# New duration estimates for TensorE and ScalarE in a kernel that orders its own instructions

## The chip, the cores and the metric

The kernel runs on one core of one Trainium2 chip, in one launch. The metric is the device time of a launch in microseconds (us). TensorE (PE) does the matrix products, VectorE (DVE), ScalarE (ACT) and GpSimd (POOL) the elementwise work, and SyncE (SP) issues the transfers. Each engine works through its own instructions in the order in which they were emitted, so an instruction that waits holds up all that stands behind it on its engine.

## The reference, cut to what matters

One layer of a hybrid encoder runs over 1104 rows: 16 meta rows and 1024 frames of a prompt, and 64 rows of a second request group with a cache of 272 rows. D_MODEL is 1024, D_FF 2816.

```
x = x + 0.5 * (silu(rmsnorm(x) @ wg) * (rmsnorm(x) @ wu)) @ wd     # feed-forward 1
p = rmsnorm(x) @ w_in                                              # one projection, split among the heads
# group A: gated DeltaNet, 4 heads: short convolution + silu, l2-normalised q and k,
#   per chunk: u = solve(I + a, rhs); o = eg*(q@m0) + (q k^T * decay)@u; m = exp(g)*m0 + k^T@u
# group B: latent attention, 4 heads: cq = rmsnorm(p_q) @ w_uq, c = rmsnorm(p_kv), rotary parts,
#   keys and values from c @ w_ukv, softmax over a block-causal mask
x = x + concat(A, B) @ w_out
x = x + 0.5 * (silu(rmsnorm(x) @ wg) * (rmsnorm(x) @ wu)) @ wd     # feed-forward 2
y = rmsnorm(x)                                                     # final norm
```

All inputs and outputs are float32.

## The kernel before

**Numbers.** A float32 product is made of three passes over operands that are cut in a high part and a remainder (names that end in h and l, as wh and wl): high by high, remainder by high, high by remainder. ScalarE casts the high part, VectorE subtracts to get the remainder. The rows of x are handled in four blocks of 276 columns or three of 384, 384 and 336. In the feed-forwards the products go by a scheme of seven products for eight (class `Seven`): sums and differences of two pairs of weight blocks and of two pairs of activation blocks (tiles `raw`, `wx`; `s`, `st`) are formed by VectorE first, and TensorE's results are added up into several banks' worth of output (`sn`, `hb`).

**Stages.** Feed-forward 1: `norm_pair` prepares the activations of pair 0 and pair 1 while the first weights arrive, then the gate and up products run (`half_steps`, in cycles of 14 blocks of 12 products with 276 columns), their silu product `hb` is written to DRAM (`hd`) and comes back, split, as `XH` and `XL` for the products with wd. Then a norm (`norm_chunk`), the combined projection head by head (`head_proj`), the delta rule in groups of three chunks (`gdn_group`, tiles like `Zg`, `Tpg`, `T2g`, `Ung` and the state `M`), the latents (`proj_latent`), the queries (`mla_queries`, `query_rope` with tile `qt`), attention (`mla_attend`), the out projection (`out_proj`), feed-forward 2, and the final norm (`final_chunk`, with output tile `fy`).

**What sets the order.** All of these are generators that are registered as tasks with a rank. `Tasks.step` (L468) emits a piece of one task at a time: the first task in order of rank whose planned ready time is not later than the planned time of TensorE, or, if none is ready, the one that gets ready first. The planned times come from `Clock`: `note` (L361) is called after every operation (all are issued from one line, L424, by `Timed`), takes the operands' planned ends plus a latency, and adds `cost` (L351), an estimate of its duration by engine and number of elements. `lag` and `complete` give a task the planned time at which a tile is ready, so a task can ask to go on when it is. Tiles are taken from rings of buffers, and a planned time is kept for when each comes free. Nothing of this exists when the kernel runs: the plan only decides in which order the instructions stand on each engine, and semaphores do the waiting.

Each name carries a number in the order of allocation (`raw_165`, `bk_14159`; `bk` is a bank of PSUM). The numbers differ between the two kernels even where the work is the same. Group tiles carry head and group: `Tpg00` is head 0, group 0.

Of the kernel before, what the change touches and what calls it, by code (L numbers as in the profile page):

```python
# [9 lines left out]
F32R = mybir.dt.float32r  # L10
# [302 lines left out]
class Clock:  # L313
# [37 lines left out]
    def cost(self, eng, op, out, ins):  # L351
        n = max(math.prod(x.shape[1:]) for x in ins + [out])
        if eng == "tensor":
            n = math.prod(out.shape[1:])
            k = 2 if self.at["tensor"] < 6.8 else 1
            if op == "transpose":
                return 0.11 * k
            return k * (max(0.107, n * 0.00042) if ins[-1].dtype == F32R else 2 * max(0.107, n * 0.00084))
        return {"vector": 0.07 + n * 0.00105, "scalar": 0.13 + n * 0.00075, "gpsimd": 0.15 + n * 0.0022}[eng]

    def note(self, eng, op, args, kw):  # L361
        aps = [x for x in list(args) + list(kw.values()) if hasattr(x, "tensor")]
# [2350 lines left out]
```

## Time and profile before

| what | value |
|---|---|
| time, median of 3 runs | 2364.56 us (2363.49 to 2367.12) |
| the profiled execution's own time | 2365.06 us |
| its span | 2363.3 us |
| PE busy | 2299.7 us, 97%, 16356 instructions |
| DVE busy | 1511.4 us, 64%, 3499 instructions |
| ACT busy | 926.4 us, 39%, 2038 instructions |
| POOL busy | 204.3 us, 9%, 488 instructions |
| chain that ended last | PE 85%, DVE 9%, ACT 2%, DMA 2% |
| transfers | 214.29 MB, 91 GB/s on the mean |

The span is that of the profiled execution on the chip; busy is the time in which at least one instruction of an engine is recorded. TensorE is busy for all but 63.6 us of the span. The granted clock of TensorE was 0.985 of full speed over the span. Matmuls are pipelined, so the duration in a row is that from start to result, and a single product shows more (290 ns) than the distance at which products follow each other.

### The profile page before, as it was taken

The page shows a single profiled execution, that of the slowest core. Times are in us where ns is not written, and L with a number is a line of the kernel's source. Part 1 is how long each engine was busy: PE and PEld are TensorE (multiplying, and loading weights), DVE is VectorE, ACT ScalarE, POOL GpSimd, SP SyncE. Part 2 cuts the span into 40 slices and gives each one's busy share as a digit, 9 for nine tenths or more (in the row PEclk, how much of TensorE's full clock was granted, in tenths as well). Part 3 has the DMA queues.
Part 4 walks back from the last instruction along what each step waited for, and adds up shares of the span by engine and source line. Part 5 has one row for each costly group of instructions (what it writes and reads, how often), then busy time and mean ns, then how long its engine had stood idle before and what let it go on. Part 6 is the DMA issues. An engine that isn't in the chain of part 4 may idle for free.

```text
span 2363.3 us, 41362 instructions
## 1 busy us (share of the span) xinstructions
PE 2299.7 (97%) x16356; PEld 2273.8 (96%) x16356; DVE 1511.4 (64%) x3499; ACT 926.4 (39%) x2038; POOL 204.3 (9%) x488
## 2 busy tenths in 40 slices
PE   9999999999999999899998999899999999999998
PEld 8999999999999899899998998899999999999998
DVE  7844554575766767788867566567544554657676
ACT  5433333352112445555533555334333333441123
POOL 0000000000000403323245000000000000000002
PEclk9999999999999999999998999999999999999999
DMA  6322222362421331112122103623222222444212
GB/s 199 112 78 83 83 69 70 101 206 97 142 92 37 114 92 40 55 38 66 36 73 66 45 16 91 194 91 107 80 75 83 83 66 73 147 160 147 87 56 76
DMA packets 231043, 214.29 MB, mean 91 GB/s; under 512 B 18372, under 2 KB 202864, under 8 KB 230848
## 3 DMA queue, kind: packets, MB, share of 16 engines
q1 hardware_dynamic: 230832, 211.64, 28.4%
q8 instruction: 128, 2.10, 0.4%
q14 instruction: 67, 0.55, 0.1%
q10 hardware_dynamic: 16, 0.00, 0.0%
HBM read 159.05 MB, written 52.55 MB: 90 GB/s over the span
## 4 chain that ended last, share of the span: by engine, by line
PE 85%; DVE 9%; ACT 2%; DMA 2%; issue 1%; POOL 1%; SPq 0%; DVEq 0%; ACTq 0%; POOLq 0%
PE bk L424 85%; DVE s L424 1%; DVE cv L424 1%; DVE wl L424 1%; DVE rs_q L424 1%; DMA X<-in_w_out_dram 1%; DVE rs_r L424 0%; ACT wh L424 0%; POOL rs_q L424 0%; ACT s L424 0%; DMA s<-in_w_out_dram 0%; DVE st L424 0%; ACT pp L424 0%; POOL tkq L424 0%; DMA wx<-in_ffn_wg_dram 0%
## 5 line engine op out<-in xcount | busy, mean ns | idle before, releaser
L424 PE MATMUL bk<-s,wh 128*128 128x276 f32 x3136 | 600.9, 290 | 4.9 <-ACT sn L424 2.3
L424 PEld LDWEIGHTS bk<-s,wh 128*128 128x128 f32 x3136 | 492.9, 188 | 6.3 <-ACT sn L424 2.5
L424 PE MATMUL bk<-s,wl 128*128 128x276 f32 x1568 | 449.3, 290 | 1.6 <-DVE wl L424 1.6
L424 PE MATMUL bk<-s,wx 128*128 128x276 f32 x2964 | 394.0, 290 | 1.7 <-DVE s L424 1.7
L424 PEld LDWEIGHTS bk<-s,wx 128*128 128x128 f32 x2964 | 383.5, 188 | 1.9 <-DVE s L424 1.9
L424 DVE SCALAR_TENSOR_TENSOR R<-bk,R 128x384 f32<-128x384 f32 (+1 forms) x480 | 230.6, 533 | 133.4 <-PE bk L424 133.1
L424 PEld LDWEIGHTS bk<-s,wl 128*128 128x128 f32 x1568 | 293.3, 188 | 2.3 <-DVE wl L424 2.3
L424 DVE TENSOR_TENSOR sn<-bk,sn 128x276 f32<-128x276 f32 x237 | 105.1, 444 | 207.5 <-PE bk L424 203.5
L424 ACT COPY sn<-bk 128x276 f32<-128x276 f32 x237 | 92.0, 389 | 243.3 <-PE bk L424 239.2
L424 PE MATMUL bk<-XH,wh 128*128 128x384 f32 (+1 forms) x576 | 166.9, 344 | 0.0
L424 PE MATMUL bk<-XL,wh 128*128 128x384 f32 (+1 forms) x576 | 161.5, 334 | 0.0
L424 PE MATMUL bk<-XH,wl 128*128 128x384 f32 (+1 forms) x576 | 161.5, 334 | 0.0
L424 DVE TENSOR_TENSOR raw<-wx,raw 128x512 f32<-128x512 f32 x40 | 27.6, 691 | 155.1 <-DMA raw<-in_ffn_wu_dram 155.1
L424 ACT CAST wh<-wx 128x512 fp32r<-128x512 f32 (+1 forms) x89 | 76.4, 858 | 100.5 <-DVE wx L424 87.7
L424 DVE TENSOR_TENSOR wx<-raw,wx 128x512 fp32r<-128x512 f32 (+2 forms) x149 | 112.0, 755 | 4.9 <-ACT wx L424 4.8
L424 ACT ACTIVATE sn<-sn 128x276 f32<-128x276 f32 x158 | 68.5, 435 | 117.0 <-DVE sn L424 116.9
L424 PEld LDWEIGHTS bk<-XH,wh 128*128 128x128 f32 x576 | 105.8, 191 | 0.0
L424 PEld LDWEIGHTS bk<-XL,wh 128*128 128x128 f32 x576 | 105.8, 191 | 0.0
L424 PEld LDWEIGHTS bk<-XH,wl 128*128 128x128 f32 x576 | 105.4, 191 | 0.0
L424 DVE TENSOR_TENSOR wl<-raw,wh 128x512 fp32r<-128x512 f32 (+4 forms) x95 | 89.8, 949 | 13.5 <-ACT wh L424 13.4
L424 ACT CAST wh<-raw 128x512 fp32r<-128x512 f32 (+4 forms) x95 | 77.1, 814 | 52.0 <-PE bk L424 28.7
L424 DVE TENSOR_TENSOR wl<-wx,wh 128x512 fp32r<-128x512 f32 (+1 forms) x89 | 87.2, 980 | 12.2 <-ACT wh L424 12.2
(436 smaller groups left out, 4465.3 us busy)
## 6 DMA issues: line engine op xcount, KB each, us to landing
raw<-in_ffn_wu_dram SPq DMA_DIRECT2D x102, 256.0 KB, 4.5
wx<-in_ffn_wg_dram SPq DMA_DIRECT2D x49, 512.0 KB, 4.0
hd<-hb SPq DMA_DIRECT2D x88, 276.0 KB, 2.2
raw<-in_ffn_wd_dram SPq DMA_DIRECT2D x40, 512.0 KB, 4.7
XH<-hd SPq DMA_DIRECT2D x24, 552.0 KB, 3.7
XL<-hd SPq DMA_DIRECT2D x20, 552.0 KB, 4.6
xa<-x SPq DMA_DIRECT2D x16, 552.0 KB, 5.3
raw<-in_w_in_dram SPq DMA_DIRECT2D x16, 512.0 KB, 4.1
```

What stands on the lines that cost most here:

```text
L424: r = f(*args, **kw)
```

## The change

Two lines in `Clock.cost` are altered: for a product with one operand in the fast float32 format, n columns were put at max(0.107, 0.00042 n) us and are now put at max(0.112, 0.0087 + 0.000435 n); for a plain float32 product the floor goes from 0.107 to 0.112, taken twice; an operation of ScalarE with n elements goes from 0.13 + 0.00075 n to 0.14 + 0.00082 n. The estimates of VectorE (0.07 + 0.00105 n), GpSimd, the transfers and all latencies stay.

```
             if op == "transpose":
                 return 0.11 * k
-            return k * (max(0.107, n * 0.00042) if ins[-1].dtype == F32R else 2 * max(0.107, n * 0.00084))
-        return {"vector": 0.07 + n * 0.00105, "scalar": 0.13 + n * 0.00075, "gpsimd": 0.15 + n * 0.0022}[eng]
+            return k * (max(0.112, 0.0087 + n * 0.000435) if ins[-1].dtype == F32R else 2 * max(0.112, n * 0.00084))
+        return {"vector": 0.07 + n * 0.00105, "scalar": 0.14 + n * 0.00082, "gpsimd": 0.15 + n * 0.0022}[eng]
```

The instructions are the same but for a few small products of TensorE that fill the first microseconds (14276 rows before, 14283 now). Their order changes on every engine. Three pieces of it follow, each of before and of now.

VectorE at the start, where the second pair of activations (`s112`, `s113`) is made, before:

```order
127 L424 TENSOR_TENSOR wx2_144<-wx3_145,wx1_143 128x512
128 L424 TENSOR_TENSOR raw_165<-wx3_145,raw_164 128x512
129 L424 TENSOR_TENSOR s112_1258<-st1_116,s15_1206 128x1104
130 L424 TENSOR_TENSOR sn_1237<-bk_1187,sn_1237 128x276
131 L424 TENSOR_TENSOR sn_1251<-bk_1210,sn_1251 128x276
132 L424 TENSOR_TENSOR raw_164<-raw_164 128x512
133 L424 TENSOR_TENSOR wl_163<-wx3_145,wh_162 128x1024
134 L424 TENSOR_TENSOR s113_1291<-st0_115,s16_1260 128x1104
```

and now:

```order
127 L424 TENSOR_TENSOR wx2_144<-wx3_145,wx1_143 128x512
128 L424 TENSOR_TENSOR s112_1227<-st1_116,s15_1158 128x1104
129 L424 TENSOR_TENSOR s113_1259<-st0_115,s16_1229 128x1104
130 L424 TENSOR_TENSOR sn_1243<-bk_1193,sn_1243 128x276
131 L424 TENSOR_TENSOR sn_1257<-bk_1209,sn_1257 128x276
132 L424 TENSOR_TENSOR raw_165<-wx3_145,raw_164 128x512
133 L424 TENSOR_TENSOR raw_164<-raw_164 128x512
134 L424 TENSOR_TENSOR wl_163<-wx3_145,wh_162 128x1024
```

Both activations have moved ahead of the subtraction of raw_164 from wx3_145, a pair of loaded weights.

ScalarE at the end of the gate and up products of feed-forward 1, where the last weights (rA2, rL2) and the first blocks for wd (XH0) come in, before:

```order
335 L424 ACTIVATE sn_4747<-sn_4747 128x276
336 L424 ACTIVATE sn_4767<-sn_4767 128x276
337 L424 CAST wh_158<-rA2_4960 128x1024
338 L424 CAST XH0_4962<-raw_165 128x512
339 L424 CAST XH0_4962<-wx3_145 128x512
340 L424 CAST wx0_142<-raw_164 128x512
341 L424 COPY sn_4988<-bk_4975 128x276
342 L424 COPY sn_5007<-bk_4994 128x276
343 L424 COPY sn_5022<-bk_4975 128x276
```

and now:

```order
339 L424 ACTIVATE sn_4774<-sn_4774 128x276
340 L424 CAST wx0_142<-raw_164 128x512
341 L424 COPY sn_4992<-bk_4979 128x276
342 L424 COPY sn_5011<-bk_4998 128x276
343 L424 COPY sn_5025<-bk_4979 128x276
...
347 L424 CAST XH0_4972<-raw_165 128x512
348 L424 CAST XH0_4972<-wx3_145 128x512
349 L424 CAST wx0_142<-raw_165 128x512
350 L424 COPY sn_5104<-bk_5091 128x276
351 L424 CAST wh_162<-rA2_4970 128x1024
```

The cast from rA2 has moved behind the copies from the banks, ten places down.

VectorE in a cycle of the dense steps of feed-forward 1, where `hb` empties two banks and `raw_165<-wx3_145,raw_164` is the first subtraction of a new block of weights, before:

```order
182 L424 TENSOR_TENSOR wl_161<-raw_164,wh_160 128x512
183 L424 TENSOR_TENSOR wl_161<-wx3_145,wh_160 128x512
184 L424 TENSOR_TENSOR wx3_145<-wx3_145 128x512
185 L424 TENSOR_TENSOR hb_1752<-bk_1612,sn_1625 128x276
186 L424 TENSOR_TENSOR hb_1768<-bk_1632,sn_1645 128x276
187 L424 TENSOR_TENSOR wx2_144<-raw_165,wx1_143 128x512
188 L424 TENSOR_TENSOR wx2_144<-wx3_145,wx1_143 128x512
189 L424 TENSOR_TENSOR wx0_142<-raw_164,wx0_142 128x512
190 L424 TENSOR_TENSOR raw_165<-wx3_145,raw_164 128x512
```

and now:

```order
204 L424 TENSOR_TENSOR wx2_144<-raw_165,wx1_143 128x512
205 L424 TENSOR_TENSOR wx2_144<-wx3_145,wx1_143 128x512
206 L424 TENSOR_TENSOR sn_1875<-bk_2016,sn_1875 128x276
207 L424 TENSOR_TENSOR raw_165<-wx3_145,raw_164 128x512
208 L424 TENSOR_TENSOR raw_164<-raw_164 128x512
209 L424 TENSOR_TENSOR wl_163<-wx3_145,wh_162 128x1024
210 L424 TENSOR_TENSOR hb_1980<-bk_1844,sn_1857 128x276
211 L424 TENSOR_TENSOR wx0_142<-raw_165,wx0_142 128x512
212 L424 TENSOR_TENSOR hb_1996<-bk_1862,sn_1875 128x276
```

The first subtraction of the new block and the wide low part behind it (`wl` of 1024 columns) now stand ahead of the two evacuations `hb<-bk`, where they stood behind them; the subtractions for `wx2` have moved ahead of it all, among the adds into `sn`.

Elsewhere, in words: in the delta rule of head 0, group 0, TensorE has 57 products of 336 columns between its product from `Zg00` and the first from `Tpg00`, where it had 24, and VectorE has one convolution (`cv`) less between the two. At the last solve (head 3, group 2) products of the latents now stand between the steps of the solve (6 between those with `Tfg` and `Xg`, 9 up to `T2g`, 9 up to `U2g`, 6 up to `Ung`), where 18 products of the queries stood in one place and none in the others; 3, 6, 9 and then no query products follow between the steps of the state `M`. In the final norm, where 48 small transposes stood behind the last product of feed-forward 2, 36 of them now stand ahead of its last 12 products.

## Rows read from the trace of the kernel before

**Rows 1.** Stretches of the span: us, busy us (xcount) of each engine, PEclk, DMA, GB/s.

```profile
110.00:455.00 345.00, 345.00 (x2709) 345.00 (x2708) 175.44 (x328) 129.28 (x258) 0.00 (x0) 1.00 0.25 76
800.00:1000.00 200.00, 190.32 (x1196) 187.16 (x1195) 139.54 (x429) 100.16 (x252) 53.61 (x120) 0.94 0.20 61
1000.00:1250.00 250.00, 247.10 (x1781) 243.70 (x1780) 196.83 (x713) 123.47 (x370) 85.60 (x248) 0.99 0.17 52
1250.00:1320.00 70.00, 60.15 (x384) 55.69 (x384) 49.57 (x169) 29.34 (x84) 30.79 (x65) 0.88 0.26 78
```

**Rows 2.** Timeline of PE: start, us, instruction [idle before, what ended it].

```profile
107.29 1.66 PE L424 MATMUL bk<-s,wx 128*128 128x276 f32 x11 [1.71 <-DVE s L424]
462.95 0.53 PE L424 MATMUL bk<-s,wh 128*128 128x276 f32 x2 [2.25 <-ACT sn L424]
908.44 0.82 PE L424 MATMUL bk<-Tpg,V32g 128*128 128x32 f32 x3 [2.91 <-DVE Tpg L424]
978.63 0.49 PE L424 MATMUL bk<-M,wTg 128*128 128x128 f32 x2 [1.46 <-DVE M L424]
1254.36 0.99 PE L424 MATMUL bk<-ident,ong 128*128 128x128 f32 x3 [2.76 <-ACT ong L424]
1264.27 0.94 PE L424 MATMUL bk<-T2g,ATg 128*128 128x128 f32 x6 [0.43 <-DVE T2g L424]
1268.67 0.50 PE L424 MATMUL bk<-ident,qt 80*128 80x80 f32 x4 [3.46 <-POOL qt L424]
```

**Rows 3.** The page's groups: busy us, mean ns, idle time before.

```profile
L424 DVE TENSOR_TENSOR sn<-bk,sn 128x276 f32<-128x276 f32 x237 | 105.1, 444 | 207.5 <-PE bk L424 203.5
L424 ACT COPY sn<-bk 128x276 f32<-128x276 f32 x237 | 92.0, 389 | 243.3 <-PE bk L424 239.2
L424 DVE TENSOR_TENSOR raw<-wx,raw 128x512 f32<-128x512 f32 x40 | 27.6, 691 | 155.1 <-DMA raw<-in_ffn_wu_dram 155.1
```

**Rows 4.** Timeline of DVE at the start.

```profile
105.33 0.69 DVE L424 TENSOR_TENSOR raw<-wx,raw 128x512 f32<-128x512 f32 x1 [5.02 <-DMA raw<-in_ffn_wu_dram]
105.93 1.30 DVE L424 TENSOR_TENSOR s<-st,s 128x1104 fp32r<-128x1104 f32 x1
```

**Rows 5.** Timeline of ACT at the end of feed-forward 1.

```profile
460.01 1.05 ACT L424 CAST wh<-rA 128x1024 fp32r<-128x1024 f32 x1 [4.46 <-DMA rA<-in_ffn_wg_dram]
462.53 0.67 ACT L424 COPY sn<-bk 128x276 f32<-128x276 f32 x2
```

**Rows 6.** Waits, by tile: us in total, times, longest us.

```profile
DVE raw L424 <- DMA raw<-in_ffn_wu_dram: 155.9, 36, 5.5
```

**Rows 7.** Timeline of DVE in one dense step.

```profile
256.25 0.68 DVE L424 TENSOR_TENSOR raw<-raw 128x512 f32<-128x512 f32 x1
256.85 1.22 DVE L424 TENSOR_TENSOR wl<-wx,wh 128x1024 fp32r<-128x1024 f32 x1
265.04 0.45 DVE L424 TENSOR_TENSOR hb<-bk,sn 128x276 f32<-128x276 f32 x1 [0.52 <-PE bk L424]
271.66 0.69 DVE L424 TENSOR_TENSOR raw<-wx,raw 128x512 f32<-128x512 f32 x1 [4.37 <-DMA raw<-in_ffn_wu_dram]
```

**Rows 8.** Timeline of DVE ahead of the first Tpg.

```profile
904.65 3.16 DVE L424 SCALAR_TENSOR_TENSOR cv<-ext,vec,cv 128x339 f32<-128x339 f32 x3
908.02 0.28 DVE L424 STREAM_TRANSPOSE Tpg<-Upg 128x96 f32<-128x96 f32 x1
```

**Rows 9.** Timeline of PE, then of DVE, at the end.

```profile
2353.24 2.35 PE L424 MATMUL bk<-ident,XH 128*128 128x128 f32 x20
...
2354.84 3.37 DVE L424 TENSOR_SCALAR fy<-bk,fr 128x512 f32<-128x512 f32 x5
```

**Rows 10.** Stretches of 40 us, columns as in Rows 1.

```profile
840.00:880.00 40.00, 40.00 (x234) 39.95 (x233) 26.32 (x91) 19.12 (x36) 5.60 (x16) 0.91 0.27 82
880.00:920.00 40.00, 37.09 (x219) 36.80 (x218) 27.70 (x86) 21.83 (x59) 14.18 (x27) 0.87 0.25 75
1240.00:1280.00 40.00, 32.45 (x212) 30.94 (x211) 27.29 (x101) 13.16 (x40) 22.02 (x59) 0.83 0.24 74
```

## The prediction

> **What bounds the kernel now.** The page comes first: PE is busy for 2299.7 of 2363.3 us, so a change that only moves work can win at most the 63.6 us in which TensorE stands still, and can lose as much as it opens anew. The stretches of the span say where these 63.6 us lie [rows 1]. In the dense feed-forward steps PE is busy for 345.00 of 345.00 us; the delta-rule stage leaves 9.7 us (200 less 190.32), the next 250 us only 2.9 and the end of the mixer 9.9 (70 less 60.15). Then the timeline of PE, whose brackets hold the idle time ahead of an instruction and what ended it: I look for gaps at places where the two orders differ [rows 2]. The rest of the trace is read to see why each of those gaps was there.
>
> **What the change can do.** It adds and removes no work: the planner emits the same operations with other guesses at their time, and what can change is the order on each in-order engine. The guesses come nearer to the trace for TensorE and ScalarE only. A 276-column product takes 345.00/2709 = 0.127 us [rows 1]; its estimate was 0.116 and becomes 0.129. The ScalarE copy of 276 columns takes 0.389 [rows 3]; its estimate goes from 0.337 to 0.366. VectorE's stays: the 276-column add is put at 0.36 and takes 0.444, the 512-column one at 0.608 and takes 0.691 [rows 3]. So one error is mended and another stands out more: beside a TensorE that is now planned at its pace, VectorE is planned 12 to 19% too fast.
>
> [...]
>
> **Part by part.** The gaps in turn, as the changed order treats them.
>
> 1. Start, pair 1: 1.71 us ahead of the product at 107.29, ended by VectorE [rows 2]. VectorE sat 5.02 us on a transfer for `raw<-wx,raw` at 105.33, and the normalised activations `s<-st,s` that PE wanted stood behind it, from 105.93 [rows 4]. In the new order both `s` stand ahead of that `raw`, which alone waits: -1.7. What is late next is the subtraction itself, by the 2 × 0.65 us of the two `s`, for weights used later.
>
> 2. End of the first feed-forward: 2.25 us ahead of 462.95, ended by the ScalarE copy `sn` [rows 2]. ScalarE waited 4.46 us for the transfer into rA, did four casts (460.01 to 462.53), and only then copied the bank that PE needed [rows 5]. Now the copies stand ahead of that cast, and the load is issued earlier. -2.25.
>
> 3. The 36 dense steps. VectorE waits there for the weights of wu, 155.9 us in 36 waits, 4.33 each, the longest 5.5 [rows 6]; in the order before, the two evacuations `hb<-bk` stand ahead of this wait (265.04 before the next one), now they stand behind it [rows 7]. A cycle of 14 blocks of 12 products is 14 × 1.53 = 21.4 us. In the new order the subtractions `wx2`, which free the buffer to be loaded, end at about 17; with 4.9 us for issue and load the wait ends 0.5 us into the next cycle. Behind it stand its own subtraction and one more (0.6 each, from start to start), the wide `wl` (1.2, and 0.5 until ScalarE's cast is there) and the first evacuation (0.45), done at 3.9; the product that needs its bank opens the fifth block, at 4 × 1.53 = 6.1: 2.2 us to spare. The longest wait is 1.2 over the mean, so the cover holds: 0. It can't be a gain, PE has no idle time there. If the cover is gone, the later half of the landings, late by 0.6 on average, cost 18 × 0.6 = +11. I take 0, since 1.2 is half of 2.2.
>
> 4. First group of the delta rule: 2.91 us ahead of 908.44, ended by `Tpg` [rows 2]. VectorE did two convolutions (`cv`) before it came to `Tpg`, at 908.02 [rows 8]. In the new order one of them has gone to another place and the square root starts at once; TensorE has 57 products of 336 columns between Zg and Tpg instead of 24, 33 × 0.155 (0.127 × 336/276) = 5.1 us more, of which 1.6 are work taken from there (u1). So +3.5 us of cover for 2.91 of idle: -2.9. Bounds: 0, if VectorE's convolution only moves the wait on, to -2.9.
>
> 5. Last solve and the queries. 2.76 us ahead of 1254.36 (ong) and 0.43 ahead of 1264.27 (T2g) [rows 2]: 6 to 9 products of the latent projection now stand between the steps of the solve, where there were none: -2.8 and -0.4. But these products were cover elsewhere. The three state steps behind the solve now have 3, 6, 9 and 0 query products between them; a state step with little beside it waited 1.46 us at 978.63 [rows 2]: +1.5, between 0 and 3 × 1.46 = 4.4. And the transpose of `qt` waited 3.46 for POOL with 2.1 to 3.1 us of work ahead of it; it now has 1.7, so 0.4 to 1.4 more: +1.0.
>
> 6. Heads 1 to 3, 1000 to 1250. Steps of the chain come 5 to 15 us of TensorE work sooner. There are 2.9 us of idle time in all [rows 1] and hardly anything to win; each step that comes sooner can stand before its operand. Two thirds of a gap like that at 978.63: +1.0, from -2.9 to +9.2 (below).
>
> 7. Tail. PE's work ends with transposes, the last till 2355.6; `fy` on VectorE follows from 2354.84 [rows 9]. Of the 48 transposes behind the last product 36 now stand ahead of the last 12 products. The amount is the same, but the chain behind the last product (residual, square, sum, square root) starts later by 36 × 0.118 (2.35/20) = 4.2 us, and only the few `fy` of the last block are left behind it, instead of 3.37 us of them on VectorE and waits for TensorE in between: +0.5, from -1 to +2.
>
> Attention, the output projection and the norm chunk are emitted almost alike; their gaps stay, with ±2.
>
> Sum: -1.7 - 2.25 - 2.9 - 2.8 - 0.4 = -10.05; +1.5 + 1.0 + 1.0 + 0.5 = +4.0; together -6.05. The profiled execution took 2365.06 us (1.8 around its span), which gives 2359.0; the median of the runs lay 0.5 below it: **2358.5 us**.
>
> **Rivals.**
>
> A. The gaps come back. TensorE gets past a wait sooner and meets the next one sooner: behind 908.44 the stage to 1000 leaves 6.8 us idle, paced by VectorE, and at 1250 to 1320 the queries hang on POOL. For it speaks that in the delta rule the solves form one chain and that 940 to 1000 has no filler in either order; against it that the gaps at the start and at 462.95 are followed by hundreds of us without one [rows 1]. If only those two stay won: 2365.06 - 3.95, and the 4.0 of new gaps: 2365.1, median 2364.6: no change.
>
> B. Slower: VectorE's estimates, left too small, decide. The place is 1000 to 1250. There before's two errors (TensorE 9% too fast, VectorE 12 to 19%) partly made up for each other and the idle share was 1%; with one mended, steps are put ahead of their operands. The price is that of the neighbouring stage, where chains wait openly: 9.7 per 200 us is 12.1 in 250, 9.2 more than now; and the granted clock, 0.94 there and 0.99 here [rows 1], costs up to 0.05 × 250 = 12.5. With the wins of steps 1, 2 and 4 (-6.9) this makes +2.3 to +14.8, in the middle 2373. It decides from some 10 us of idle time in that stretch on. Against it: the steps have more filler around them than those from 940 to 1000.
>
> [...]
>
> That the change does nothing is part of A: the orders differ on every engine, but PE's work is dense where they differ most.
>
> **How the numbers follow.** Forecast 0.40, A 0.28, B 0.24, C 0.08. A measurement of this kernel tells 0.2% from no change, 4.7 us: faster is below 2359.8, slower above 2369.3. The forecast's own range is 2353 to 2361, of which some 0.85 is faster; A lies between 2361 and 2370, nine tenths of it the same; B between 2367 and 2379 (+2.3 and +14.8), four fifths slower; C all faster. Faster: 0.40 × 0.85 + 0.08 = 0.42. Slower: 0.24 × 0.8 and a tenth of A, 0.22. The rest, 0.36, is the same. With a tenth left out at either end the range is 2349.5 to 2370.5: it holds the forecast and A, the upper part of C and the lower end of B.
>
> **What would show it.** Right: no idle time at the first products of pair 1 (near 107) nor at the first gate block of the last weights (near 460), `Tpg` of the first group without a wait, and VectorE's waits for wu still near 4.3 us each with PE busy throughout from 110 to 455. Wrong: idle time in front of each dense step (step 3), or a stretch from 1000 to 1250 with over 10 us of idle time (B), or the same sum of idle time at other places (A). If the idle time falls by more than the time does, or less, the granted clock of 800 to 1320 has moved.

## The result and the profile after

The changed kernel takes **2379.46 us** (median of 5 runs, 2376.0 to 2381.22); the kernel before, on the same chip, 2367.12 (5 runs, 2363.49 to 2367.91). The ratio is 1.0059, with a 95% interval of 1.0044 to 1.0073: slower by 0.6%, where I had forecast 2358.5 and had 2370.5 as the upper end. TensorE works as long as before (2303.0 us against 2299.7) in a span that is 15.4 us longer (2378.7 against 2363.3).

The stretches of the span of after, with the columns of [rows 1] (stretch, its length, busy us of PE, PEld, DVE, ACT, POOL, then TensorE's granted clock, DMA share and GB/s):

```profile
110.00:455.00 345.00, 345.00 (x2710) 345.00 (x2709) 176.92 (x330) 123.15 (x260) 0.00 (x0) 1.00 0.25 76
455.00:490.00 35.00, 34.73 (x274) 34.52 (x273) 23.88 (x43) 16.20 (x32) 0.00 (x0) 1.00 0.69 204
800.00:1000.00 200.00, 192.83 (x1245) 189.28 (x1246) 140.31 (x438) 100.73 (x251) 53.01 (x122) 0.97 0.20 61
1000.00:1250.00 250.00, 243.02 (x1742) 238.09 (x1741) 198.63 (x725) 122.37 (x371) 82.77 (x240) 0.99 0.17 53
1250.00:1320.00 70.00, 62.62 (x415) 57.49 (x414) 46.05 (x150) 32.26 (x90) 31.23 (x72) 0.95 0.25 75
...
1480.00:1530.00 50.00, 37.47 (x261) 36.48 (x260) 24.28 (x43) 19.36 (x31) 0.00 (x0) 0.86 0.70 197
1530.00:1660.00 130.00, 119.96 (x896) 118.35 (x895) 81.10 (x167) 37.98 (x58) 0.00 (x0) 0.93 0.29 88
```

and of before, for 455 to 490 and for the two stretches that the prediction had not looked at:

```profile
455.00:490.00 35.00, 31.31 (x232) 30.87 (x232) 25.43 (x45) 16.83 (x33) 0.00 (x0) 0.95 0.50 154
1480.00:1530.00 50.00, 41.14 (x284) 39.93 (x283) 26.27 (x42) 21.32 (x34) 0.00 (x0) 0.90 0.76 214
1530.00:1660.00 130.00, 127.47 (x1003) 126.58 (x1003) 86.91 (x181) 44.59 (x70) 0.00 (x0) 1.00 0.32 98
```

Length less PE's busy time is its idle time. From 800 to 1320, where the prediction looked, it is 21.5 us in all against 22.4 in [rows 1] (9.7, 2.9 and 9.9): shifted among the three, and nearly the same in sum. The loss is further back. The output projection and the second norm (1480 to 1530) go from 8.9 to 12.5 us idle, and the end of the projection and the start of feed-forward 2 (1530 to 1660) from 2.5 to 10.0, with the clock at 0.93 instead of 1.00. Over 5 us at a time the clock of after is 0.77 from 1595 to 1600, 0.54 from 1600 to 1605, 0.98 from 1610 to 1615, 0.50 from 1615 to 1625, and 1.00 in the rest of the stretch. Near 1602 TensorE begins a group of three products of 276 columns every 0.69 us (1599.62 to 1603.76), and near 1610, at 1.00, every 0.385 us (1609.30 to 1611.61). My estimate from the 0.93 is a cost of at most 0.07 × 130 = 9 us, beside the idle time.

The same is read from how far after is behind at an equal count of TensorE's products (those of 200 columns or more, 13741 in each kernel): it is 1.5 us ahead at 1480, where attention is done (points are given by the time in before), 2.4 behind at 1520, past the first gap of the output projection, 15.1 behind at 1652, and its span ends 15.4 later. Feed-forward 2's dense part and everything after it are as fast as before.

One caution on such readings: two executions are not equal even where the order is the same. After and e3 (below) have the same order on every engine up to the edit near the end of the output projection, and yet at 1480 e3 is 4.2 us ahead where after is 1.5 ahead; e1 and e7, alike in the same way, are 0.5 and 6.1 ahead there. Their idle times in the stretches from 800 to 1320 agree within 0.6 us; the granted clock does not (1250 to 1320: 0.93 in e1, 0.98 in e7). So the idle times can be compared, but being ahead or behind by up to some 6 us at 1480, in one trace of each kernel, is no finding on the order.

### The profile page after: what moved, and what is told of

The parts are those of the page before. It is cut to its first block, busy times and chain, and to the rows that moved or that the text cites. A ratio compares the mean times of both kernels' runs of the same rounds, so it can differ in the third digit from the quotient of the medians.

```text
span 2378.7 us, 41321 instructions
## 1 busy us (share of the span) xinstructions
PE 2303.0 (97%) x16354; PEld 2270.9 (95%) x16354; DVE 1510.8 (64%) x3499; ACT 912.5 (38%) x2038; POOL 202.6 (9%) x488
## 4 chain that ended last, share of the span: by engine, by line
PE 82%; DVE 9%; ACT 3%; DMA 3%; issue 2%; POOL 1%; SPq 0%; DVEq 0%; ACTq 0%; POOLq 0%
PE bk L424 82%; DVE s L424 2%; DVE rs_q L424 1%; DVE wl L424 1%; DMA wx<-in_ffn_wg_dram 1%; DVE cv L424 1%; DMA s<-oT 1%; DVE st L424 1%; ACT s L424 0%; DVE rs_r L424 0%; POOL rs_q L424 0%; DMA s<-in_w_out_dram 0%; DMA s<-x 0%; SPq L424 0%; ACT pp L424 0%
## 5 line engine op out<-in xcount | busy, mean ns | idle before, releaser
L424 ACT CAST wx<-raw 128x512 fp32r<-128x512 f32 (+1 forms) x111 | 76.4, 692 | 73.6 <-PE bk L424 61.3
L424 DVE TENSOR_TENSOR wl<-raw,wh 128x512 fp32r<-128x512 f32 (+4 forms) x96 | 90.0, 941 | 17.8 <-ACT wh L424 17.8
```

The lines of the kernel that those rows point to most:

```text
L424: r = f(*args, **kw)
```

## Where the time went, by the traces

TensorE's timeline of after (start, us, instruction, and in brackets the idle time ahead of it and what ended it), from 1480 to 1625:

```profile
1492.90 0.60 PE L424 MATMUL bk<-cTh,wh 128*128 128x276 f32 x1 [7.38 <-ACT wh L424]
...
1588.95 0.91 PE L424 MATMUL bk<-s,wh 128*128 128x276 f32 x4 [2.25 <-ACT s L424]
...
1597.96 0.83 PE L424 MATMUL bk<-s,wh 128*128 128x276 f32 x2 [2.56 <-ACT wh L424]
...
1616.42 0.83 PE L424 MATMUL bk<-s,wh 128*128 128x276 f32 x2 [2.17 <-ACT wh L424]
1619.50 0.60 PE L424 MATMUL bk<-s,wl 128*128 128x276 f32 x1 [2.25 <-DVE wl L424]
```

There are two places of loss.

**The output projection (the gap of 7.38 us).** TensorE's row of before at this place:

```profile
1490.21 0.39 PE L424 MATMUL bk<-cTh,wh 128*128 128x276 f32 x1 [3.16 <-ACT wh L424]
```

The gap was 3.16 us long there. It waits for `wh`, a weight of w_out that ScalarE casts. ScalarE's timeline of after:

```profile
1485.88 1.20 ACT L424 CAST s<-s 128x552 fp32r<-128x552 f32 x2 [1.88 <-DMA s<-oT]
1490.70 1.20 ACT L424 CAST s<-s 128x552 fp32r<-128x552 f32 x2 [3.62 <-DMA s<-oT]
1491.81 1.04 ACT L424 CAST wh<-X 128x1024 fp32r<-128x1024 f32 x1
1492.76 1.04 ACT L424 CAST wh<-raw 128x1024 fp32r<-128x1024 f32 x1
```

and of before:

```profile
1487.29 1.21 ACT L424 CAST s<-s 128x552 fp32r<-128x552 f32 x2 [1.67 <-DMA s<-oT]
1489.11 1.05 ACT L424 CAST wh<-X 128x1024 fp32r<-128x1024 f32 x1 [0.61 <-DMA X<-in_w_out_dram]
1490.82 1.05 ACT L424 CAST wh<-raw 128x1024 fp32r<-128x1024 f32 x1 [0.66 <-DMA raw<-in_w_out_dram]
1492.34 1.21 ACT L424 CAST s<-s 128x552 fp32r<-128x552 f32 x2 [0.48 <-DMA s<-oT]
```

In after one more cast of activations stands ahead of the two `wh`, and its transfer from `oT` lands at 1490.7; the weights, which before took as they came at 1489.1, wait behind it until 1491.8. One pair of casts has changed places with one other. The gap is 4.2 us longer: 2.7 of these are the later start of the first `wh` cast (1491.81 instead of 1489.11), and the other 1.5 are those by which TensorE reached this place sooner.

**The start of feed-forward 2 (the gaps from 1588 to 1620).** VectorE's timeline of after:

```profile
1574.30 1.31 DVE L424 TENSOR_TENSOR s<-X 128x1104 f32<-128x1104 f32 x1 [13.21 <-PE bk L424]
1575.53 0.79 DVE L424 TENSOR_TENSOR s<-bk,s 128x276 f32<-128x276 f32 x2
...
1597.94 1.22 DVE L424 TENSOR_TENSOR wl<-wx,wh 128x1024 fp32r<-128x1024 f32 x1 [0.48 <-ACT wh L424]
```

and of before:

```profile
1567.79 0.44 DVE L424 TENSOR_TENSOR s<-bk,s 128x276 f32<-128x276 f32 x1
...
1572.28 1.31 DVE L424 TENSOR_TENSOR s<-X 128x1104 f32<-128x1104 f32 x1 [2.83 <-PE bk L424]
...
1591.43 1.21 DVE L424 TENSOR_TENSOR wl<-wx,wh 128x1024 fp32r<-128x1024 f32 x1
```

VectorE stands still for 13.2 us instead of 2.8, ahead of one subtraction, `s<-X` of 1104 columns. It makes the tile s04 (`X3` in `norm_pair`), the difference from which an operand of the seven products is cut, for pair 0 of the second feed-forward. Its sources are ready; what it waits for is its *buffer*, which holds the weight of the fifth of the eight output blocks until TensorE has done that block's products for the last two column blocks; in both kernels the semaphore value that s04 waits for is that of the last product which reads this weight. Behind it stand the residual adds `s<-bk,s` of banks that TensorE has finished, the subtractions for the next weights, and, through ScalarE, the casts that TensorE wants at 1588 to 1620. VectorE and ScalarE then work the rest off in turn, and TensorE runs into one gap after another, at a granted clock of 0.86 from 1580 to 1640 (in before 1.00).

Why it waits longer is in the order of VectorE, before (s19, s112, s110, s14 are residuals, two adds for each block of the projection):

```order
2421 L424 TENSOR_TENSOR s110_17564<-bk_17695,s110_17564 128x276
2422 L424 TENSOR_TENSOR s14_17570<-bk_17696,s14_17570 128x276
...
2428 L424 TENSOR_TENSOR s19_17563<-bk_17797,s19_17563 128x276
2429 L424 TENSOR_TENSOR s112_17569<-bk_17798,s112_17569 128x276
2430 L424 TENSOR_TENSOR s09_17883<-st2_17215,s02_17839 128x1104
2431 L424 TENSOR_TENSOR s04_17885<-X0_16428 128x1104
```

and after:

```order
2421 L424 TENSOR_TENSOR s110_17567<-bk_17662,s110_17567 128x276
2422 L424 TENSOR_TENSOR s14_17573<-bk_17663,s14_17573 128x276
2423 L424 TENSOR_TENSOR s09_17766<-st2_17214,s02_17724 128x1104
2424 L424 TENSOR_TENSOR s04_17768<-X0_16428 128x1104
2425 L424 TENSOR_TENSOR s110_17567<-bk_17740,s110_17567 128x276
2426 L424 TENSOR_TENSOR s14_17573<-bk_17741,s14_17573 128x276
```

Before, s04 comes behind the fourth pair of adds, so that only one block of products is missing; now behind the second, and three are missing, of 48 products or some 6 us each. The planner can't see this: a tile's reuse counts only reads that have been emitted already, and the reads by the blocks to come have not. By the new line a block of 48 products is planned at 6.2 us, by the old one at 5.6; so fewer blocks fit beside the chain of norms, and s04 is emitted two blocks sooner. That TensorE's estimate moves s04 is shown below (e1, e2, e5); that it does so by the length of a block is my reading of the planner.

## The experiments

All were timed in 5 rounds beside the kernel before; each ratio is to it on the same chip, with its 95% interval (e1 to e4, e5 to e8 and e9 to e12 ran on three chips). s04's wait is VectorE's idle time ahead of that subtraction; ahead and behind are against before, at equal counts of products of 200 columns or more.

### One half of the change each

Only TensorE's lines are new (e1): against after, ScalarE's estimate is put back.

```
-        return {"vector": 0.07 + n * 0.00105, "scalar": 0.14 + n * 0.00082, "gpsimd": 0.15 + n * 0.0022}[eng]
+        return {"vector": 0.07 + n * 0.00105, "scalar": 0.13 + n * 0.00075, "gpsimd": 0.15 + n * 0.0022}[eng]
```

> Only TensorE's two estimates are new, ScalarE's are those of before. Theory 1 (two places carry the loss: at the start of feed-forward 2 VectorE's write of s04 stands before the residual adds and waits for TensorE, some 13 us; in the out projection a cast of weights stands behind a cast that waits for a transfer, some 4 us): here s04 stands as early as in the changed kernel, the weight cast of the out projection as in the kernel before, so VectorE waits about 13 us ahead of s04, and the time is 2367 + 13 - 2 = about 2377, with a gap near 1490 of 3 to 4 us instead of 7.4. Rival (ScalarE's longer estimates are what moves the casts and the adds): about 2367, no wait of 13 us. Rival B of the prediction (VectorE too short in the plan): also slower, but by idle time spread over 1000 to 1250.

Measured: 2377.7 us, 1.0051 (1.0038 to 1.0063).

```profile
1569.29 1.31 DVE L424 TENSOR_TENSOR s<-X 128x1104 f32<-128x1104 f32 x1 [11.96 <-PE bk L424]
```

The long wait is there, and s04 stands behind the second pair of adds. This kernel is 3.2 us ahead at 1520 and 9.1 behind at 1652, after the start of feed-forward 2: TensorE's estimate alone makes the second loss, and not the one in the output projection (7.5 us idle there from 1480 to 1530, before 8.9).

Only ScalarE's is new (e2): against after, TensorE's estimate is put back.

```
-            return k * (max(0.112, 0.0087 + n * 0.000435) if ins[-1].dtype == F32R else 2 * max(0.112, n * 0.00084))
+            return k * (max(0.107, n * 0.00042) if ins[-1].dtype == F32R else 2 * max(0.107, n * 0.00084))
```

> Only ScalarE's estimate is new. Theory 1: s04 stands behind the fourth pair of residual adds, as before, and the casts of the out projection too: VectorE's wait there stays near 3 us and the time is that of before, 2367 +- 4. Rival (ScalarE's estimates): near the changed kernel's, 2376 to 2381.

Measured: 2370.3 us, 1.0022 (1.0014 to 1.0031). s04 waits 2.76 us behind the fourth pair of adds, as before, and nothing is lost at feed-forward 2. From 1480 to 1530 it is 10.0 us idle, where before is 8.9, e1 7.5 and after 12.5: neither estimate alone makes the loss of the output projection, only both together do. The kernel is 3.3 us behind already in feed-forward 1 and 4.3 at 1480, so ScalarE's estimate costs elsewhere, by other moves, which I didn't trace. Whether the losses of 0.51% and 0.22% add up to after's 0.59% can't be told: their sum of 0.73% lies at the upper end of after's interval.

### Taking s04's buffer only when it is near

After, with tiles s04, s05 and s06 taken only once the fifth, sixth and seventh block of the last two column blocks has been emitted (the planner holds the task until then); the hold of s04:

```
     B11, B21, B12, B22 = raws
-    X3, X4 = x.new(4), x.new(5)
+    yield 0, hold(4)          # hold(i): when block i of cs (2, 3) has been emitted
+    X3 = x.new(4)
...
+        s.blocks_out[len(cs), at] = nc.at["tensor"]     # in the output projection, behind a block
```

> The changed kernel, and the three tiles of pair 0 in feed-forward 2 (s04, s05, s06) are only taken when the products of the out projection that read their buffers have been emitted. [...] Rival (the loss sits in the weights' loads and casts at the start of feed-forward 2, not in s04): the gaps ahead of the casts wh stay, 2375 to 2380.

Measured: 2369.18 us, 1.0015 (1.0005 to 1.0025).

```profile
1530.00:1660.00 130.00, 124.78 (x958) 123.97 (x957) 83.45 (x165) 42.56 (x68) 0.00 (x0) 0.97 0.31 94
```

s04 waits for nothing, the stretch is 5.2 us idle instead of 10.0 and its clock 0.97 instead of 0.93. Of after's 12.7 us lost at the start of feed-forward 2, 5.0 are left (1.1 ahead at 1520 to 3.9 behind at 1652), so the hold takes more than half of the loss and not all. The time lies just above the 2366 to 2368 that I had expected. The gap in the output projection stays, at 6.20 us.

### And the casts of the output projection later

The same, with the activations' casts counted as landing 1 us later, so that the weights' casts come first:

```
-                    yield nc.lag(o)
+                    yield nc.lag(o) + 1.0
```

> As e3, and the plan lets the casts of the out projection's activations wait 1 us more for their load, which puts the weights' cast ahead of the fifth of them, as it stood before. Theory 1: the gap of 7.4 us near 1490 falls to about 3, with its share of the clock another 4 us: 2361 to 2364, below the kernel before by what the changed order wins at the start, at 463 and in the delta rule. Rival (the load of the weights itself is late there): as e3.

Measured: 2366.37 us, 1.0001 (0.9992 to 1.0009): the time of before, and not the 2361 to 2364 expected. The gap has gone down to 1.97 us, and ScalarE's casts of `wh` stand ahead again:

```profile
1484.33 1.05 ACT L424 CAST wh<-X 128x1024 fp32r<-128x1024 f32 x1 [0.62 <-DVE X L424]
1486.08 1.05 ACT L424 CAST wh<-raw 128x1024 fp32r<-128x1024 f32 x1 [0.70 <-DMA raw<-in_w_out_dram]
1487.62 1.21 ACT L424 CAST s<-s 128x552 fp32r<-128x552 f32 x2 [0.49 <-DMA s<-oT]
```

The two edits together take away the whole loss while the new estimates stay. The second one's share is not clear of noise: its interval overlaps that of e3 alone. Nor is the start of feed-forward 2 free of loss: 2.8 us are still lost there (4.5 ahead to 1.7 ahead).

### The estimate half way

TensorE's line half way between old and new, ScalarE's old: `max(0.109, 0.0043 + n * 0.0004275)`.

> TensorE's estimate half way (0.122 us for 276 columns, between 0.116 and 0.129), ScalarE's as before. s04 then stands behind the third pair of residual adds: one pair later than in e1, one earlier than in the kernel before. Theory 1: VectorE waits there by about one block of out projection (6 us) less than in e1, some 7 us, and about half of e1's loss is left: 2369 to 2373. Rival (the loss is no matter of that place, but of TensorE's plan being longer everywhere): idle time spread, and also about 2371, but with the wait ahead of s04 not near 7.

Measured: 2376.65 us, 1.0043 (1.0029 to 1.0057).

```profile
1574.85 1.31 DVE L424 TENSOR_TENSOR s<-X 128x1104 f32<-128x1104 f32 x1 [7.37 <-PE bk L424]
```

s04 now stands behind the third pair of adds, and its wait is one block shorter than after's 13.2, near the 7 us expected. But the time is above the range expected, and the loss at feed-forward 2 is 10.4 us (3.1 behind to 13.5), not half of e1's 12.3: how long s04 waits doesn't give the loss by itself. The order behind it differs too; what that costs I didn't trace.

### Rival B: VectorE's estimate raised

After, with VectorE's fixed part raised to what two row durations give: `"vector": 0.155 + n * 0.00105`.

> The changed kernel with VectorE's estimate at 0.155 + 0.00105 n, which is the duration of its adds in the trace, not their distance (0.36 us at 276 columns, as the old estimate says). Theory 1: a longer VectorE plan puts s04 back behind the fourth pair of adds: its wait falls to about 3, the start of feed-forward 2 costs nothing; in the out projection half a cast stands ahead of the weights' cast, 1 to 2 us: 2364 to 2370. Rival B: VectorE was too short in the plan all over, so the idle time from 1000 to 1250 falls from 6.8 to below 4 as well, and the time to 2360 or below. Rival (that an estimate above the distance is wrong makes all elementwise work late): over 2372.

Measured: 2401.3 us, 1.0144 (1.0124 to 1.0164). The stretches:

```profile
800.00:1000.00 200.00, 186.15 (x1198) 182.49 (x1196) 137.31 (x422) 101.21 (x251) 56.84 (x123) 0.96 0.21 60
1000.00:1250.00 250.00, 237.97 (x1653) 234.27 (x1653) 182.78 (x651) 116.20 (x343) 73.87 (x198) 0.96 0.17 49
```

If too small an estimate of VectorE were the trouble, the delta rule should have become denser. It has 13.9 and 12.0 us of idle time, nearly twice after's, and the kernel is 24 us behind at 1480. So raising the estimate isn't the cure that B's mechanism asks for, and "too small" was wrong to begin with (below). What this run does confirm is s04's part. It stands behind the fourth pair of adds again:

```profile
1596.31 1.31 DVE L424 TENSOR_TENSOR s<-X 128x1104 f32<-128x1104 f32 x1 [2.83 <-PE bk L424]
```

It waits as long as in before, and nothing more is lost at the start of feed-forward 2 (24 us behind on either side of it).

### The hold with one half, and on before

e1 with the hold; and before with the hold, as a control.

> e1 with the hold of e3: TensorE's numbers new, ScalarE's old, s04 to s06 taken only when their buffers' readers have been emitted. Theory 1: e1 less its 9 to 12 us at the start of feed-forward 2, and its out projection is already without the gap of 7 us: 2364 to 2368, the same as before or a little under. Rival (the hold only trades the wait): above 2372.

Measured: **2358.56 us**, 0.9968 (0.9956 to 0.9981), the fastest of all, and below the range expected.

```profile
1530.00:1660.00 130.00, 128.84 (x1016) 128.34 (x1016) 88.02 (x173) 47.18 (x77) 0.00 (x0) 1.00 0.33 98
```

The start of feed-forward 2 is 1.2 us idle, at full clock; e1's 12.3 us lost there have become a gain of 2.3. The hold is the only edit against e1, and the two ratios are 0.83% apart. Of the 17.8 us between the two traces 14.6 arise there, where the hold acts; the other 3.2 arise ahead of it, where the orders are the same, and are not its work.

> The kernel before with the hold alone. Theory 1: there s04 waits only 2.8 us, so nothing is to be won: 2364 to 2368, within 0.2% of before. Rival (the hold is a gain by itself, whatever the estimates): 2357 or below, and then e3's gain says nothing of the changed order.

Measured: 2364.65 us, 0.9996 (0.9987 to 1.0005). Where s04 waits 2.8 us the hold is worth nothing that can be measured, so the hold is no gain by itself.

### How far the result hangs on the numbers

Four more with the hold, to see whether better estimates make a better order. ScalarE's put at the pace of its pairs (`0.04 + n * 0.00088`); TensorE's half way; and TensorE's slope of 0.000435 raised and lowered by 0.7% (0.000438 and 0.000432).

> e7 with ScalarE's estimate at the distance of its operations (0.04 + 0.00088 n: 0.28 us at 276 columns, 1.01 at 1104, as pairs of them follow each other in the trace). If estimates should be distances: no worse than e7, 2354 to 2361. Rival (the order is a matter of chance, any other numbers give another gap somewhere): anywhere from 2357 to 2372, with the casts of the out projection standing behind loads again (there one weights' cast now stands behind two more casts of activations, 4 us): about 2364.

> e5 with the hold. Theory 1: e5 less its loss at the start of feed-forward 2 (7 to 9 us): 2366 to 2369, no better than before, since up to 1480 e5 was 2 to 4 us behind. Rival (half the correction of TensorE gives half of e7's gain): 2361 to 2363.

> e7 with TensorE's slope 0.7% higher (0.000438), a change without meaning. If e7's gain comes from TensorE planned at its own pace: within 3 us of e7, 2356 to 2362. Rival (chance): up to 6 us away, 2362 to 2368.

> e7 with TensorE's slope 0.7% lower (0.000432). As e11: within 3 us of e7, 2356 to 2362, or by the rival up to 6 us away.

Measured, beside e7's 2358.56:

| kernel | us | ratio (95%) | where it falls behind e7 |
|---|---|---|---|
| e9, ScalarE by its pace | 2392.95 | 1.0117 (1.0102 to 1.0131) | delta rule to attention: 11.7 us idle in 1000 to 1250, 11.8 in 1320 to 1480 |
| e10, TensorE half way | 2372.36 | 1.0034 (1.0022 to 1.0046) | 6 us by 1520, 7 more at feed-forward 2 |
| e11, slope +0.7% | 2375.3 | 1.0040 (1.0028 to 1.0052) | mixer: 11.9 us idle in 1000 to 1250 |
| e12, slope -0.7% | 2366.52 | 1.0009 (1.0000 to 1.0017) | mixer: 9.6 us in 1000 to 1250, 11.6 in 1250 to 1320 |

Only e12 lies in a range expected (the rival's); the other three are slower than any range had it. e10 limits what the hold can explain: it is e5 with the hold, s04 waits for nothing, and 5.1 us are lost at the start of feed-forward 2 all the same (e5: 10.4), with gaps of 2.03 us at 1598.3 and 1.49 at 1608.9. Its interval overlaps e5's, so the hold's gain isn't clear there.

A change of 0.7% in one estimate, less than either side of the diff is off by (0.116 and 0.129 us planned for a product of 276 columns, 0.127 measured), takes the ratio from 0.9968 to 1.0009 and 1.0040, that is 10 to 17 us. So e7's gain over before is not a proof of better estimates: its order in the mixer is a good one among many, and how much of the 0.3% is luck stays open, as does what exactly makes e9's and e11's mixers slow, which I didn't trace through. Even one order has its spread: the 12 runs of e11 go from 2365.32 to 2380.99 us.

## Why the prediction was wrong, point by point

**The step that failed** is the sentence without a number of its own: "Attention, the output projection and the norm chunk are emitted almost alike; their gaps stay, with ±2." The start of feed-forward 2, where most was lost, stands neither in it nor in a numbered step, so it was put at nothing without a reason. From 1480 to 1652 after went from 1.5 us ahead to 15.1 behind: 16.6 us, against ±2. Of these 3.9 lie before 1520, with the `wh` casts, and 12.7 behind it, with s04, of which holding s04 back won 7.7 (e3); the rest I didn't trace. Two moves were enough to make most of it: one pair of casts on ScalarE, one subtraction on VectorE. What I asked of the other moves I didn't ask of these, namely what the moved instruction itself waits for. I went only to gaps. At the start of feed-forward 2 there was hardly one in before that the change could close, and the one of 3.16 us at 1490.21, longer than all but one in [rows 2], I passed over. A wait that is covered (s04's 2.83 us on VectorE) is as much a place to look at as a gap.

Of the numbered steps, TensorE's timeline of after shows:

```profile
63.79 0.92 PE L424 MATMUL bk<-dg,ones 128*128 128x40 f32 x6 [1.00 <-DVE dg L424]
...
100.16 0.52 PE L424 MATMUL bk<-s,wh 128*128 128x276 f32 x2 [0.66 <-ACT sn L424]
...
461.65 0.52 PE L424 MATMUL bk<-s,wh 128*128 128x276 f32 x2 [0.27 <-ACT sn L424]
...
983.42 1.46 PE L424 MATMUL bk<-Tpg,V32g 128*128 128x32 f32 x6 [3.40 <-DVE Tpg L424]
...
1017.88 0.49 PE L424 MATMUL bk<-M,wTg 128*128 128x128 f32 x2 [1.34 <-DVE wTg L424]
...
1256.55 1.07 PE L424 MATMUL bk<-Ung,ktg 128*128 128x128 f32 x6 [1.88 <-ACT Ung L424]
...
1267.15 0.79 PE L424 MATMUL bk<-ident,qt 80*128 80x80 f32 x4 [1.15 <-POOL qt L424]
```

- Step 1 (-1.7): the gap at 107.29 of [rows 2] is gone, but 63.79 and 100.16 have come in its place; the first 110 us hold 6.8 us of idle time, in before 6.1. Nothing was won.
- Step 2 (-2.25): right; 0.27 is left, and the clock from 455 to 490 is 1.00 instead of 0.95. At equal counts after goes from 0.7 us behind at 455 to 2.3 ahead at 600, so some 3.0 were won.
- Step 3 (0): right; PE is busy for 345.00 of 345.00 us, as in [rows 1], with the wait for wu ahead of the evacuations.
- Step 4 (-2.9): the first `Tpg` comes without a wait, as worked out; a later one has a gap of 3.40 (983.42). From 800 to 1000 there are 2.5 us less of idle time, so the size is nearly right.
- Step 5 (-0.7 in sum): the waits at 1254.36 and 1264.27 are gone, and `Ung` and `qt` bring new ones (1.88 and 1.15), as expected; from 1250 to 1320 the idle time goes from 9.9 to 7.4 us.
- Step 6 (+1.0): mis-sized, with the mechanism right: 1000 to 1250 goes from 2.9 to 7.0 us, within its bound of +9.2, with waits like that for `wTg` at 1017.88.
- Step 7 (+0.5): right; after is 15.4 us behind at the end of the span and was 15.1 behind at 1652.

Together they left after 1.5 us ahead at 1480, where the sum had some 6, and e3, in the same order, 4.2: rival A's mechanism, some of the gaps coming back elsewhere, in a size that one trace does not give. Rival B had the sign and nearly the size (2373), for a wrong reason: its stretch has 7.0 us of idle time, short of the 10 from which it was to decide, and e6 speaks against its cause. Rival C, with a chance of 0.08, counted on a higher granted clock where gaps go. After's row for one of the stretches in [rows 10]:

```profile
880.00:920.00 40.00, 39.71 (x267) 39.24 (x266) 32.26 (x97) 23.30 (x62) 14.38 (x28) 1.00 0.26 76
```

Where the gap of 880 to 920 went (2.91 us idle in before, 0.29 in after), the clock rose from 0.87 to 1.00; from 840 to 880, where PE is busy for 40.00 of 40.00 us in after too, it stayed at 0.91. Behind s04 gaps opened, and from 1530 to 1660 it fell from 1.00 to 0.93. In that stretch a lower clock stands beside more idle time in four kernels (10.0 us idle at 0.93 in after, e3's 5.2 at 0.97, before's 2.5 and e7's 1.2 at 1.00), but e6 has 6.7 at 0.99 and e11 2.1 at 0.96, and the stretch from 840 to 880 shows the lower level without a gap. So what sets the clock was not shown, and the upper part of C, which took my range down to 2349.5, rested on an estimate: no run shows how much time the clock gives back when a gap goes. Of the 12.7 us lost at feed-forward 2, 7.5 are more idle time in that stretch; my estimate is that the other 5 are the clock, within the 9 us worked out above from its 0.93.

## What to carry to other kernels

In a kernel whose planner sets the order, a better estimate is not a better order: its model's gaps (here, buffers whose last reads are not emitted yet) may have been hidden by the old numbers. So when estimates change, list for each in-order engine the instructions that have moved ahead of others, ask of each what it waits for, its buffer included, and what stands behind it, also where TensorE has no gap so far. And before a gain from such numbers is believed, try their neighbours: if a 0.7% step moves the time more than the gain, the gain is that of one order.

## What I had not expected of the hardware

In these traces a row's duration is not an engine's pace. One add of 276 columns on VectorE takes 0.44 us (1567.79 above) and two in a row 0.79 (1575.53), so the second begins some 0.35 us behind the first; one add overlaps the next by 0.09. Two casts of 1024 columns on ScalarE begin 0.95 us apart (1491.81 and 1492.76) and take 1.04 each. The old estimate of VectorE, 0.36 for 276 columns, is the pace, and my premise that VectorE was planned 12 to 19% too fast compared a pace with a duration. The 0.155 us of e6 came from durations too: 0.691 and 0.444 in [rows 3] differ by 0.247 us over 236 columns, which leaves 0.155 without columns. By start to start, the subtraction of 512 columns takes 0.60 (105.33 to 105.93 in [rows 4]) and the add of 276 columns 0.35, which leaves 0.06, where the planner has 0.07. (The two differ in more than columns: the add reads a bank of PSUM.) For ScalarE at 1024 columns the old line gives 0.13 + 1024 × 0.00075 = 0.898 and the new one 0.14 + 1024 × 0.00082 = 0.980, so that the pace of 0.95 lies between the two. At 276 columns both lines, 0.337 and 0.366, are above the pace: two copies in a row take 0.67 ([rows 5]) and one 0.389, so the second begins some 0.28 behind the first. There the change went away from the pace, not towards it; e9, which is planned with the pace there, was slower still, so nearness to the pace did not decide either.
